# A hybrid attention and DeltaNet layer on one core: PSUM banks by turns, the solve in quarters, rotation tables in the keys, TensorE in source order in the heads

## Chip, core and metric

The kernel runs on one core of one Trainium2 chip. Times are device microseconds of that core. A core has five engines that run side by side and wait for each other by semaphores: TensorE (PE; its weight loads are shown as PEld), VectorE (DVE), ScalarE (ACT), GpSimd (POOL) and SyncE (SP), whose queue issues all DMAs here.

## What is computed

One decoder layer for 512 tokens of width 2048, all in float32:

```python
h = rms_norm(x, norm_w) * (1.0 + scale) + shift        # scale, shift, gate from silu(c) @ w_ada
aq, ak, av, ag, d_qkv, dz, db, da, mg_a, mg_b = split(h @ w_in)
# windowed attention: 32 query heads, 4 key heads of 64, rotation of the first 16 channels, sinks
y_a = (swa_attention(rope(norm(aq)), rope(norm(ak)), av, sinks) * silu(ag)) @ w_o_swa
# gated DeltaNet: 16 key heads, 32 value heads of 128, chunks of 64
dq, dk, dv = split(causal_conv_silu(d_qkv, conv_w))
t_inv = triangular_solve(eye + L, eye)                 # L = strict lower part of (beta k) k^T * decay
v_new = t_inv @ v_beta - (t_inv @ k_beta_decayed) @ S  # scan over chunks, state S
y_b = (rms_norm(o, dn_norm_w) * silu(dz)) @ w_o_dn
out = x + gate * ((sigmoid(mg_a) * y_a + sigmoid(mg_b) * y_b) @ w_out)
```

## The kernel before

It is written in a tile language: the program is a sequence of instructions in source order, and a planner puts each engine's instructions in an order of its own. It takes, of the instructions whose inputs it believes ready by its own estimate of times, the earliest in the source; it also picks the buffer of a pool that it believes free first. On the chip each engine then runs its list in that fixed order and waits where something is not ready. An explicit order between two instructions of one engine can be added (the method `behind` does that for single instructions).

Stages, in order, with their rough place in the profile: startup (norm and adaLN, first projections, to 130 us), **keys** (`delta_keys`: 12 more key tiles of the DeltaNet and 18 tiles of its output gate z, to about 535), **attention** (to about 1100), **heads** (`delta_heads`: 16 groups of one q tile, two v tiles and in seven of them a z tile, with the scans, to about 2000), and the **tail** (six 2048-wide products done by a seven-product scheme).

A *channel tile* (`channel_tile`) is 128 channels of `h @ w_in`: 16 steps of three matmuls of 512 columns (`mm3`, L276 to L278: high and low halves of the float32 operands) into one PSUM bank that `product_bank` gives. Weights come as 1 MB DMAs (`raw`), ACT rounds them (`whi`, L68) and DVE takes the rest (`wlo`, L69). Before, the pool `pmm` has two banks and the planner picks which one a tile gets; in the tail `pmm` and a second pool of two alternate.

All other work is in generators. `pump` is called after every second step of a channel tile, so eight times a tile. It advances them: a *live* generator yields the number of calls until its next step; a *paced* one gets a budget per call and yields what its next step costs. The names used later:

- `keys` (per key head): convolution by ACT (L650) and three DVE steps (L653, the last reader of the bank, `y`), transposes `ptk`, norm, transposes `ptkT`, ACT copy `kT` (L765), products `pkk` (L772), DVE mask times `E`. Key tiles and z tiles alternate from key 8 on.
- `z_gate`: ACT tanh into `zth` (L316), DVE product (L318, the last reader of the bank), store `z_d` (L320). `zth` has one buffer in the keys.
- `solve` (twice, for 16 heads each, paced 0.36): loads A, one DVE product over all of A (128x4096, L827), 124 DVE steps (L835, L843), eight ACT copies `atmp` with stores `ta_d`, one more product over A (L855), stores `ts_d`. At group 8 of the heads `drain_slow` runs what is left of it at once.
- `rope_tables`: sine and cosine tables by 20 DVE operations and two ACT `Sin`, run in one go at the start of attention, in whose key tiles (`key_pair`) ACT squares `ksq` for the product `kss`.
- `queries` (per group): convolution `yq`, loads of E and `kT`, transposes `ptq`, loads `qe`, `tt`, `ta`, `lab`, `ts1` (shown as `ts`), products `pqk` (L934), `py` (L942), ACT copy `Y`, products `pu`, then `scan`: per chunk `pp`, `pv`, `pod`, then transposes `pto`. `values` transposes v (`ptv`), which ACT copies to `vt`.
- `weight_sums`: sums of weight quarters for the tail on DVE (L1490), loads `q`, stores `s_d`.

Of the kernel before, what the change touches and what calls it, by code (L numbers as in the profile page):

```python
# [16 lines left out]
P = 128  # L17
# [35 lines left out]
class Layer:  # L53
# [218 lines left out]

    def mm3(self, ps, w, x, first, last):
        nc = self.nc
        (wh, wl), (xh, xl) = w, x
        nc.tensor.matmul(ps, lhsT=wh, rhs=xh, start=first, stop=False)  # L276
        nc.tensor.matmul(ps, lhsT=wh, rhs=xl, start=False, stop=False)  # L277
        self.last_mm = nc.tensor.matmul(ps, lhsT=wl, rhs=xh, start=False, stop=last)  # L278
# [43 lines left out]
    def transpose4(self, dst, src_cols):  # L322

        for c in range(4):
            self.nc.tensor.transpose(dst[:, c * P : (c + 1) * P], src_cols(c), self.ident)


    def build(self):
        tc, nc, a = self.tc, self.nc, self.a
        with ExitStack() as es:  # L330
            self.const = es.enter_context(tc.tile_pool(name="const", bufs=1))
            self.dram = es.enter_context(tc.tile_pool(name="scratch", bufs=1, space=DRAM))
            self.dnc_es = ExitStack()
            self.dnc = self.dnc_es.enter_context(tc.tile_pool(name="dnc", bufs=1, side="right"))
            self.v_d = self.dram.tile([2, P, T], F32, name="v_d")
            self.s_d = [self.dram.tile([2, 4, 2, P, 2048], F32, name=f"s_d{e}") for e in range(6)]
            self.gate_d = self.dram.tile([D], F32, name="gate_d")
# [22 lines left out]
            self.delta_keys()  # L360
            self.psc_es.close()
            self.attention()
            self.delta_heads()
            self.dnc_es.close()
# [30 lines left out]
    def startup(self, st):  # L395
# [54 lines left out]
        ada = self.pmm.tile([P, T], F32, tag="mm", name="ada")  # L450
# [94 lines left out]
        acc_ba = self.pmm.tile([P, T], F32, tag="mm", name="ba")  # L545
# [117 lines left out]
    def delta_keys(self):  # L663
# [9 lines left out]
        with ExitStack() as sa:  # L673
# [67 lines left out]
    def keys(self, wk, g, ps):  # L741
# [28 lines left out]
        for c in range(NTB):  # L770
            sl = slice(c * P, (c + 1) * P)
            nc.tensor.matmul(pk[:, c, :], lhsT=kT[:, sl], rhs=kT[:, sl], start=True, stop=True)  # L772
# [35 lines left out]
    def solve(self, wk, b, eng):  # L808
# [18 lines left out]
        self.behind(eng.tensor_tensor(out=A, in0=A, in1=nb.unsqueeze(1).to_broadcast([P, HD, HD]), op=ALU.mult))  # L827
# [27 lines left out]
        self.behind(eng.tensor_tensor(out=A, in0=A, in1=bet.unsqueeze(2).to_broadcast([P, HD, HD]), op=ALU.mult))  # L855
# [26 lines left out]
    def queries(self, wk, g, ps, st):  # L882
# [50 lines left out]
        for c in range(NTB):  # L933
            nc.tensor.matmul(pqk[:, c, :], lhsT=kT[:, sl(c)], rhs=q[:, sl(c)], start=True, stop=True)  # L934
# [5 lines left out]
        for c in range(NTB):  # L940
            for e in range(2):
                nc.tensor.matmul(py[own[1 - e], c, :], lhsT=lab[own[e], c, :], rhs=ta[own[e], c, :], start=True, stop=True)  # L942
# [4 lines left out]
        for c in range(NTB):  # L947
            nc.tensor.matmul(pu[0][0:HD, c, :], lhsT=Y[HD:P, c, :], rhs=TT[0][HD:P, c, HD:P], start=True, stop=True)
            nc.tensor.matmul(pu[1][0:HD, c, :], lhsT=Y[0:HD, c, :], rhs=ts1[0:HD, c, :], start=True, stop=True)
# [13 lines left out]
    def scan(self, wk, g, k, kT, TT, qd, M, epsq, st):  # L963
# [6 lines left out]
        for c in range(NTB):  # L970
            if c:
                pp = self.psc.tile([P, 4, P], F32, tag="sc", name="pp")[:, 0:2, :]
                nc.tensor.matmul(pp, lhsT=kT[:, sl(c)], rhs=S, start=True, stop=True)
# [8 lines left out]
            for e in range(2):  # L982
                nc.tensor.matmul(pv[:, e, :], lhsT=TT[e][:, c, :], rhs=r[:, e, :] if c else v[e][:, c, :], start=True, stop=True)  # L983
# [11 lines left out]
            if c < NTB - 1:  # L995
                nc.tensor.matmul(pd, lhsT=k[:, c, :], rhs=vs, start=True, stop=True)
            for e in range(2):
                if c:
                    nc.tensor.matmul(po[:, e, :], lhsT=qd[e][:, c, :], rhs=S[:, e, :], start=True, stop=False)
                nc.tensor.matmul(po[:, e, :], lhsT=M[e][:, c, :], rhs=vn[:, e, :], start=c == 0, stop=True)  # L1000
# [548 lines left out]
    def rope_tables(self, wk, keep):  # L1549
# [4 lines left out]
        nc.sync.dma_start(out=fr, in_=a["k_freq"])  # L1554
        ang = wk.tile([P, T], F32, tag="r1", name="ang", bufs=1)
        nc.vector.tensor_copy(out=ang, in_=posi)
        nc.vector.tensor_scalar(out=ang, in0=ang, scalar1=fr, scalar2=None, op0=ALU.mult)
        n = wk.tile([P, T], F32, tag="r2", name="turns", bufs=1)
        ni = wk.tile([P, T], I32, tag="r0", name="turni", bufs=1)
        nc.vector.tensor_scalar(out=n, in0=ang, scalar1=1.0 / (2 * math.pi), scalar2=None, op0=ALU.mult)  # L1560
        nc.vector.tensor_copy(out=ni, in_=n)
        nc.vector.tensor_copy(out=n, in_=ni)
        for part in (TWO_PI_HI, TWO_PI_MID, TWO_PI_LO):
            nc.vector.scalar_tensor_tensor(out=ang, in0=n, scalar=-part, in1=ang, op0=ALU.mult, op1=ALU.add)

        def wrap(t):
            for lim, cmp, by in ((math.pi, ALU.is_gt, -2 * math.pi), (-math.pi, ALU.is_lt, 2 * math.pi)):
                nc.vector.tensor_scalar(out=n, in0=t, scalar1=lim, scalar2=by, op0=cmp, op1=ALU.mult)
                nc.vector.tensor_tensor(out=t, in0=t, in1=n, op=ALU.add)
            nc.vector.tensor_scalar(out=t, in0=t, scalar1=3.1415925, scalar2=-3.1415925, op0=ALU.min, op1=ALU.max)  # L1570

        wrap(ang)
        self.sin = keep.tile([P, T], F32, name="sin")
        self.cos = keep.tile([P, T], F32, name="cos")
        nc.scalar.activation(self.sin, ang, AF.Sin)
        sg = keep.tile([P, 1], F32, name="sgn")
        nc.sync.dma_start(out=sg, in_=a["k_sgn"])
        nc.vector.tensor_scalar(out=self.sin, in0=self.sin, scalar1=sg, scalar2=None, op0=ALU.mult)
        nc.vector.tensor_scalar(out=ang, in0=ang, scalar1=math.pi / 2, scalar2=None, op0=ALU.add)
        wrap(ang)  # L1580
        nc.scalar.activation(self.cos, ang, AF.Sin)
# [14 lines left out]
    def attention(self):  # L1596
        tc, nc, a = self.tc, self.nc, self.a
        with ExitStack() as es:
# [47 lines left out]
    def value_tokens(self, t, i):  # L1646
        pt = self.ptp.tile([P, NTB, P], F32, tag="tp", name="ptva")
        for c in range(NTB):
            self.nc.tensor.transpose(pt[:, c, :], t[:, c * P : (c + 1) * P], self.ident)
# [5 lines left out]
    def key_pair(self, rwk, t, ps, blk, kw, kd):  # L1655
# [8 lines left out]
        nc.tensor.matmul(pss, lhsT=blk, rhs=sq, start=True, stop=True)  # L1664
# [41 lines left out]
    def scales(self, wk, sqs, blk, rs):  # L1706
# [3 lines left out]
        for c in range(NTB):  # L1710
            sl = slice(c * P, (c + 1) * P)
            for p in range(4):
                nc.tensor.matmul(pt[32 * p : 32 * p + 32, sl], lhsT=blk[:, 48:80], rhs=sqs[p][:, sl], start=True, stop=True)
# [4 lines left out]
        for c in range(NTB):  # L1718
            nc.tensor.transpose(pt[:, c, :], sb[:, c * P : (c + 1) * P], self.ident)
# [7 lines left out]
    def attend(self, wk, kd, n, mask, sink, qs, rs, sg, done):  # L1727
        nc = self.nc
        for i in range(NTB):
# [5 lines left out]
            for pp in range(2):  # L1735
# [5 lines left out]
                for j in range(2):  # L1741
                    for e, (ps, t) in enumerate(tl):
# [3 lines left out]
                        if i == 0:  # L1746
                            nc.tensor.matmul(ps[:, j, P:], lhsT=q[b, isl], rhs=kd[b, 0:P], start=True, stop=True)
                            continue
                        for u in range(2):
                            rr = slice(u * HD, (u + 1) * HD)  # L1750
                            o = u * HD
                            nc.tensor.matmul(
                                ps[rr, j, HD - o : 256 - o], lhsT=q[b, i * P + o : i * P + o + HD],
                                rhs=kd[b, (i - 1) * P + o : (i - 1) * P + o + 192], start=True, stop=True,
                            )
# [70 lines left out]
    def gate(self, wk):  # L1826
# [17 lines left out]
        for c in range(4):  # L1844
            sl = slice(c * T, (c + 1) * T)
            ps = self.ptp.tile([P, T], F32, tag="tp", name="pgate")
            nc.tensor.matmul(ps, lhsT=self.ones, rhs=acc[:, sl], start=True, stop=True)
# [88 lines left out]
```

## Time and profile before

| | |
|---|---|
| Median of 3 runs | 2913.75 us (2908.66 to 2920.05) |
| The profiled execution | 2917.7 us |
| Its span, first to last instruction | 2915.9 us |
| TensorE busy | 2797.7 us (96%) |
| DVE, ACT, POOL busy | 2218.9, 1318.3, 147.3 us |
| DMA | 776 MB, mean 266 GB/s |

Times in the profile count from the first instruction. A row of a timeline gives start, duration, engine, source line, operation, output<-inputs, shape, count and, in brackets, the idle time of the engine before it with what ended it. Matmuls are pipelined and their ends are modelled, so a busy TensorE can still be slow: the granted clock says how slow.

### The profile page before, as it was taken

Reading aid. Unit: us, or ns where it says so; the run is one execution under the profiler, and the core shown is the slowest. Engines: PE = TensorE matmul, PEld = TensorE weight load, DVE = VectorE, ACT = ScalarE, POOL = GpSimd, SP = SyncE. Lnnn points to the kernel's source line nnn. Section 1 sums busy time; section 2 is a strip of 40 time slices with the busy share of each in tenths; the row PEclk is TensorE's granted clock in tenths of the full one; section 3 lists DMA queues with packets and bytes.
Section 4 is the critical chain, followed back from the end, with each engine's and each line's share of the span. In section 5 each row is a group of like instructions: output and inputs, shape, how many; then the busy total and the mean of one; then the engine's idle time right before and its main releaser. Section 6 shows DMA issues by size and latency. Waiting matters only on the chain.

```text
span 2915.9 us, 39613 instructions
## 1 busy us (share of the span) xinstructions
PE 2797.7 (96%) x13864; PEld 2246.0 (77%) x13864; DVE 2218.9 (76%) x3582; ACT 1318.3 (45%) x2647; POOL 147.3 (5%) x124
## 2 busy tenths in 40 slices
PE   8999898899999999999998999989999999999999
PEld 6788676777777778888886777867878878788887
DVE  7877787787786778889876776768766868887876
ACT  5565342234454444444453434435544645454543
POOL 0000000010000001101100100110000000000000
PEclk9999999999999999999999999999999999999999
DMA  9889788454456558999979998876789989998865
GB/s 402 336 275 292 264 270 300 142 177 155 157 172 185 175 164 287 290 306 300 294 236 289 314 302 274 293 228 230 247 292 326 318 323 329 350 346 276 297 242 195
DMA packets 332651, 776.38 MB, mean 266 GB/s; under 512 B 88066, under 2 KB 112258, under 8 KB 287394
## 3 DMA queue, kind: packets, MB, share of 16 engines
q1 hardware_dynamic: 332452, 773.86, 79.0%
q8 instruction: 109, 1.79, 0.2%
q14 instruction: 90, 0.74, 0.1%
HBM read 588.84 MB, written 182.66 MB: 265 GB/s over the span
## 4 chain that ended last, share of the span: by engine, by line
PE 71%; DMA 11%; DVE 10%; ACT 3%; issue 3%; SPq 1%; POOL 0%; DVEq 0%; ACTq 0%; POOLq 0%
PE mm L276 12%; PE mm L278 11%; PE mm L277 11%; PE m L277 9%; PE m L278 9%; PE m L276 8%; DMA s_d<-q 2%; DVE wlo L69 2%; DMA q<-in_w_q 2%; DMA raw<-in_w_ch 1%; DMA b_d<-o 1%; DVE q L1490 1%; PE O L1815 1%; PE pv L983 1%; PE pod L1000 1%
## 5 line engine op out<-in xcount | busy, mean ns | idle before, releaser
L69 DVE TENSOR_TENSOR wlo<-raw,whi 128x1024 fp32r<-128x1024 f32 x588 | 721.4, 1231 | 336.1 <-ACT whi L68 325.5
L68 ACT CAST whi<-raw 128x1024 fp32r<-128x1024 f32 x588 | 614.9, 1051 | 722.7 <-PE m L278 346.9
L276 PE MATMUL mm<-hh,whi 128*128 128x512 f32 x2016 | 823.4, 408 | 27.3 <-DVE zth L318 8.8
L278 PE MATMUL mm<-hh,wlo 128*128 128x512 f32 x2016 | 804.7, 399 | 6.5 <-DVE wlo L69 6.5
L277 PE MATMUL mm<-hl,whi 128*128 128x512 f32 x2016 | 803.0, 398 | 0.0
L276 PEld LDWEIGHTS mm<-hh,whi 128*128 128x128 f32 x2016 | 384.9, 191 | 120.0 <-issue 22.8
L278 PEld LDWEIGHTS mm<-hh,wlo 128*128 128x128 f32 x2016 | 384.0, 190 | 92.5 <-DVE wlo L69 10.3
L277 PEld LDWEIGHTS mm<-hl,whi 128*128 128x128 f32 x2016 | 385.5, 191 | 74.6 <-issue 1.6
L1490 DVE TENSOR_TENSOR q<-q,q 128x512 f32<-128x512 f32 x384 | 277.9, 724 | 15.9 <-DMA q<-in_w_q 14.5
L800 POOL TENSOR_SCALAR_AFFINE_SELECT E<-E 128x512 f32<-128x512 f32 x64 | 56.6, 893 | 1073.8 <-DMA E<-g_rows 962.2
L843 DVE TENSOR_TENSOR A<-A,atmp 128x62 f32<-128x62 f32 (+30 forms) x124 | 108.9, 878 | 0.6
L835 DVE TENSOR_TENSOR atmp<-A 128x62 f32<-128x62 f32 (+30 forms) x124 | 107.5, 867 | 0.5
L806 ACT ACTIVATE E<-E,neg_g 128x128 f32<-128x128 f32 x256 | 80.1, 394 | 28.2 <-POOL E L800 28.2
L653 DVE SCALAR_TENSOR_TENSOR yv<-mm,convh,yv 128x511 f32<-128x511 f32 (+2 forms) x96 | 71.5, 744 | 24.6 <-ACT yv L650 23.6
L277 PE MATMUL m<-wlo,hh 128*128 128x512 f32 x192 | 77.0, 401 | 5.2 <-DVE wlo L69 5.2
L276 PE MATMUL m<-whi,hh 128*128 128x512 f32 x192 | 76.7, 401 | 2.7 <-ACT whi L68 2.7
L278 PE MATMUL m<-whi,hl 128*128 128x512 f32 x192 | 76.1, 396 | 0.0
L988 ACT ACTIVATE vs<-pv,kd 128x128 f32<-128x128 f32 x96 | 30.1, 365 | 90.5 <-PE pv L983 90.3
L277 PE MATMUL m<-wlo,f2h 128*128 128x512 f32 x160 | 62.6, 391 | 1.2 <-DVE wlo L69 1.2
L276 PE MATMUL m<-whi,f1h 128*128 128x512 f32 x160 | 62.7, 392 | 0.0
L278 PE MATMUL m<-whi,f0l 128*128 128x512 f32 x160 | 62.5, 390 | 0.0
L278 PE MATMUL m<-whi,f2l 128*128 128x512 f32 x160 | 62.4, 390 | 0.0
(431 smaller groups left out, 4774.5 us busy)
## 6 DMA issues: line engine op xcount, KB each, us to landing
raw<-in_w_ch SPq DMA_DIRECT2D x126, 1024.0 KB
q<-in_w_q SPq DMA_DIRECT2D x384, 256.0 KB
s_d<-q SPq DMA_DIRECT2D x384, 256.0 KB
raw<-s_d SPq DMA_DIRECT2D x96, 1024.0 KB
raw<-in_w_q SPq DMA_DIRECT2D x72, 1024.0 KB
wa<-in_w_ada_ss SPq DMA_DIRECT2D x32, 1024.0 KB
gw<-in_w_ada_gate SPq DMA_DIRECT2D x16, 1024.0 KB
E<-g_rows SPq DMA_DIRECT2D x64, 256.0 KB
```

The source lines that it names most:

```text
L68: h = self.nc.scalar.copy(out=hi, in_=src)
L69: l = self.nc.vector.tensor_tensor(out=lo, in0=src, in1=hi.bitcast(F32), op=ALU.subtract)
L276: nc.tensor.matmul(ps, lhsT=wh, rhs=xh, start=first, stop=False)
L277: nc.tensor.matmul(ps, lhsT=wh, rhs=xl, start=False, stop=False)
L278: self.last_mm = nc.tensor.matmul(ps, lhsT=wl, rhs=xh, start=False, stop=last)
L653: nc.vector.scalar_tensor_tensor(out=y[:, s:], in0=ps[:, : T - s], scalar=w[:, j : j + 1], in1=y[:, s:], op0=ALU.mult, op1=ALU.add)
L800: self.last_mask = self.nc.gpsimd.affine_select(out=E, in_=E, pattern=[[0, NTB], [1, P]], compare_op=ALU.is_ge, fill=NEG, base=0, channel_ ...
L806: self.nc.scalar.activation(E[:, c, :], E[:, c, :], AF.Exp, bias=self.neg_g[:, c, h : h + 1])
L835: eng.tensor_tensor(out=t, in0=A[:, m : m + 1, m + 1 :].to_broadcast([P, m, n]), in1=A[:, :m, m : m + 1].to_broadcast([P, m, n]), op=ALU.mult,
L843: self.behind(eng.tensor_tensor(out=A[:, :m, m + 1 :], in0=A[:, :m, m + 1 :], in1=t, op=ALU.add))
L988: nc.scalar.activation(vs[:, e, :], pv[:, e, :], AF.Copy, scale=self.kd[:, c, 2 * g + e : 2 * g + e + 1])
L1490: self.behind(self.nc.vector.tensor_tensor(out=q[f], in0=q[x], in1=q[y], op=ALU.add))
```

## The change

Four edits. **Banks:** the two-bank pool becomes pools of one bank that products take strictly by turns; in the tail four of them.

```diff
-            self.pmm = pm_es.enter_context(tc.tile_pool(name="pmm", bufs=2, space=PSUM, reuse_waits="tile"))
-            self.banks, self.bank_i = [self.pmm], 0
+            bank = lambda n: pm_es.enter_context(tc.tile_pool(name=f"pm{n}", bufs=1, space=PSUM, reuse_waits="tile"))
+            self.banks, self.bank_i = [bank(0), bank(1)], 0
...
-            self.banks.append(self.pmb)
+            self.banks += [bank(2), bank(3)]
```

**Solve:** the two products over A are made in four parts, each followed by a yield of 1.2 (the second alike), and the pace is 0.41.

```diff
-            self.solves = self.paced(self.solve_all(), 0.36)
+            self.solves = self.paced(self.solve_all(), 0.41)
...
-        self.behind(eng.tensor_tensor(out=A, in0=A, in1=nb.unsqueeze(1).to_broadcast([P, HD, HD]), op=ALU.mult))
+        for j in range(0, HD, 16):
+            s = slice(j, j + 16)
+            self.behind(eng.tensor_tensor(out=A[:, s], in0=A[:, s], in1=nb.unsqueeze(1).to_broadcast([P, 16, HD]), op=ALU.mult))
+            yield 1.2
```

**Rotation tables:** `sin` and `cos` get a pool of their own around keys and attention; the tables are made by a live generator in the keys that begins after 40 calls of the pump. Its steps are one or two DVE operations with yields of 2 between them; the last steps are the two ACT `Sin` and the sign.

```diff
+            rwk = sa.enter_context(tc.tile_pool(name="rwk", bufs=1, reuse_waits="tile"))
+            self.go(self.rope_tables(rwk, rwk), 40)
...
-            with ExitStack() as er:
-                rwk = er.enter_context(tc.tile_pool(name="rwk", bufs=1, reuse_waits="tile"))
-                self.rope_tables(rwk, keep)
```

**Source order:** every matmul and transpose goes through `pe`, which in the heads, and there alone, adds an order behind the instruction before it in the source on TensorE.

```diff
+    def pe(self, ins):
+        return self.tc.keep_in_program_order(ins) if self.in_order else ins
...
-        nc.tensor.matmul(ps, lhsT=wh, rhs=xh, start=first, stop=False)
+        self.pe(nc.tensor.matmul(ps, lhsT=wh, rhs=xh, start=first, stop=False))
...
+            self.in_order = True
             self.delta_heads()
+            self.in_order = False
```

More of the change, by code (lines that the diff above doesn't have):

```diff
@@ L275, in mm3 @@
         (wh, wl), (xh, xl) = w, x
-        nc.tensor.matmul(ps, lhsT=wh, rhs=xh, start=first, stop=False)
-        nc.tensor.matmul(ps, lhsT=wh, rhs=xl, start=False, stop=False)
-        self.last_mm = nc.tensor.matmul(ps, lhsT=wl, rhs=xh, start=False, stop=last)
+        self.pe(nc.tensor.matmul(ps, lhsT=wh, rhs=xh, start=first, stop=False))
+        self.pe(nc.tensor.matmul(ps, lhsT=wh, rhs=xl, start=False, stop=False))
+        self.last_mm = self.pe(nc.tensor.matmul(ps, lhsT=wl, rhs=xh, start=False, stop=last))
     def behind(self, ins, other=None):
@@ L324, in transpose4 @@
         for c in range(4):
-            self.nc.tensor.transpose(dst[:, c * P : (c + 1) * P], src_cols(c), self.ident)
+            self.pe(self.nc.tensor.transpose(dst[:, c * P : (c + 1) * P], src_cols(c), self.ident))
     def build(self):
@@ L359, in build @@
             self.sol = self.dnc_es.enter_context(tc.tile_pool(name="sol", bufs=1, side="right", reuse_waits="tile"))
-            self.delta_keys()
-            self.psc_es.close()
-            self.attention()
+            with tc.tile_pool(name="rope", bufs=1) as rope:
+                self.sin, self.cos = (rope.tile([P, T], F32, name=n) for n in ("sin", "cos"))
+                self.delta_keys()
+                self.psc_es.close()
+                self.attention()
+            self.in_order = True
             self.delta_heads()
+            self.in_order = False
             self.dnc_es.close()
@@ L449, in startup @@
         ssq = sp.tile([P, NTB], F32, name="xssq")
-        ada = self.pmm.tile([P, T], F32, tag="mm", name="ada")
+        ada = self.product_bank("ada")
         by_pe = lambda kt: int(kt % 2 == 0 or kt == KT - 1)
@@ L544, in startup @@
         acc_v = [pa.tile([P, T], F32, tag=f"x{i}", name=f"v{i}") for i in range(2)]
-        acc_ba = self.pmm.tile([P, T], F32, tag="mm", name="ba")
+        acc_ba = self.product_bank("ba")
         self.acc_k = [self.psc.tile([P, T], F32, tag="sc", name=f"k{n}") for n in range(NST)]
@@ L771, in keys @@
             sl = slice(c * P, (c + 1) * P)
-            nc.tensor.matmul(pk[:, c, :], lhsT=kT[:, sl], rhs=kT[:, sl], start=True, stop=True)
+            self.pe(nc.tensor.matmul(pk[:, c, :], lhsT=kT[:, sl], rhs=kT[:, sl], start=True, stop=True))
         nc.sync.dma_start(out=self.kT_d[g], in_=kT)
@@ L854, in solve @@
         yield 4.5
-        self.behind(eng.tensor_tensor(out=A, in0=A, in1=bet.unsqueeze(2).to_broadcast([P, HD, HD]), op=ALU.mult))
+        for j in range(0, HD, 16):
+            s = slice(j, j + 16)
+            self.behind(
+                eng.tensor_tensor(
+                    out=A[:, s], in0=A[:, s], in1=bet[:, s].unsqueeze(2).to_broadcast([P, 16, HD]), op=ALU.mult
+                )
+            )
+            yield 1.2
         for k2 in range(2):
@@ L933, in queries @@
         for c in range(NTB):
-            nc.tensor.matmul(pqk[:, c, :], lhsT=kT[:, sl(c)], rhs=q[:, sl(c)], start=True, stop=True)
+            self.pe(nc.tensor.matmul(pqk[:, c, :], lhsT=kT[:, sl(c)], rhs=q[:, sl(c)], start=True, stop=True))
         for e in range(2):
@@ L941, in queries @@
             for e in range(2):
-                nc.tensor.matmul(py[own[1 - e], c, :], lhsT=lab[own[e], c, :], rhs=ta[own[e], c, :], start=True, stop=True)
+                self.pe(nc.tensor.matmul(py[own[1 - e], c, :], lhsT=lab[own[e], c, :], rhs=ta[own[e], c, :], start=True, stop=True))
         Y = wk.tile([P, NTB, HD], F32, tag="Y", name="Y", bufs=1)
@@ L947, in queries @@
         for c in range(NTB):
-            nc.tensor.matmul(pu[0][0:HD, c, :], lhsT=Y[HD:P, c, :], rhs=TT[0][HD:P, c, HD:P], start=True, stop=True)
-            nc.tensor.matmul(pu[1][0:HD, c, :], lhsT=Y[0:HD, c, :], rhs=ts1[0:HD, c, :], start=True, stop=True)
+            self.pe(nc.tensor.matmul(pu[0][0:HD, c, :], lhsT=Y[HD:P, c, :], rhs=TT[0][HD:P, c, HD:P], start=True, stop=True))
+            self.pe(nc.tensor.matmul(pu[1][0:HD, c, :], lhsT=Y[0:HD, c, :], rhs=ts1[0:HD, c, :], start=True, stop=True))
         for e in range(2):
@@ L972, in scan @@
                 pp = self.psc.tile([P, 4, P], F32, tag="sc", name="pp")[:, 0:2, :]
-                nc.tensor.matmul(pp, lhsT=kT[:, sl(c)], rhs=S, start=True, stop=True)
+                self.pe(nc.tensor.matmul(pp, lhsT=kT[:, sl(c)], rhs=S, start=True, stop=True))
                 r = wk.tile([P, 2, P], F32, tag="r", name="r", bufs=1)
@@ L982, in scan @@
             for e in range(2):
-                nc.tensor.matmul(pv[:, e, :], lhsT=TT[e][:, c, :], rhs=r[:, e, :] if c else v[e][:, c, :], start=True, stop=True)
+                self.pe(nc.tensor.matmul(pv[:, e, :], lhsT=TT[e][:, c, :], rhs=r[:, e, :] if c else v[e][:, c, :], start=True, stop=True))
             vn = wk.tile([P, 2, P], F32, tag="vn", name="vn", bufs=2)
@@ L995, in scan @@
             if c < NTB - 1:
[L996 removed]
+                self.pe(nc.tensor.matmul(pd, lhsT=k[:, c, :], rhs=vs, start=True, stop=True))
             for e in range(2):
                 if c:
[L999 to L1000 removed]
+                    self.pe(nc.tensor.matmul(po[:, e, :], lhsT=qd[e][:, c, :], rhs=S[:, e, :], start=True, stop=False))
+                self.pe(nc.tensor.matmul(po[:, e, :], lhsT=M[e][:, c, :], rhs=vn[:, e, :], start=c == 0, stop=True))
             nc.scalar.copy(out=osb[:, :, c, :], in_=po)
@@ L1554, in rope_tables @@
         nc.sync.dma_start(out=fr, in_=a["k_freq"])
+        sg = keep.tile([P, 1], F32, name="sgn")
+        nc.sync.dma_start(out=sg, in_=a["k_sgn"])
+        yield 4
         ang = wk.tile([P, T], F32, tag="r1", name="ang", bufs=1)
@@ L1561, in rope_tables @@
         nc.vector.tensor_copy(out=ni, in_=n)
+        yield 2
         nc.vector.tensor_copy(out=n, in_=ni)
@@ L1569, in wrap @@
                 nc.vector.tensor_tensor(out=t, in0=t, in1=n, op=ALU.add)
+                yield 2
             nc.vector.tensor_scalar(out=t, in0=t, scalar1=3.1415925, scalar2=-3.1415925, op0=ALU.min, op1=ALU.max)
-        wrap(ang)
-        self.sin = keep.tile([P, T], F32, name="sin")
-        self.cos = keep.tile([P, T], F32, name="cos")
+            yield 2
+        yield from wrap(ang)
+        nc.vector.tensor_scalar(out=self.cos, in0=ang, scalar1=math.pi / 2, scalar2=None, op0=ALU.add)
+        yield from wrap(self.cos)
+        yield 3
         nc.scalar.activation(self.sin, ang, AF.Sin)
-        sg = keep.tile([P, 1], F32, name="sgn")
-        nc.sync.dma_start(out=sg, in_=a["k_sgn"])
+        nc.scalar.activation(self.cos, self.cos, AF.Sin)
+        yield 2
         nc.vector.tensor_scalar(out=self.sin, in0=self.sin, scalar1=sg, scalar2=None, op0=ALU.mult)
-        nc.vector.tensor_scalar(out=ang, in0=ang, scalar1=math.pi / 2, scalar2=None, op0=ALU.add)
-        wrap(ang)
-        nc.scalar.activation(self.cos, ang, AF.Sin)
     def rope(self, x, i):
@@ L1648, in value_tokens @@
         for c in range(NTB):
-            self.nc.tensor.transpose(pt[:, c, :], t[:, c * P : (c + 1) * P], self.ident)
+            self.pe(self.nc.tensor.transpose(pt[:, c, :], t[:, c * P : (c + 1) * P], self.ident))
         vt = self.vtok_a[:, :, i * P : (i + 1) * P]
@@ L1663, in key_pair @@
         pss = self.ptp.tile([P, T], F32, tag="tp", name="kss")
-        nc.tensor.matmul(pss, lhsT=blk, rhs=sq, start=True, stop=True)
+        self.pe(nc.tensor.matmul(pss, lhsT=blk, rhs=sq, start=True, stop=True))
         ms = rwk.tile([P, T], F32, tag="pT", name="kms", bufs=4)
@@ L1712, in scales @@
             for p in range(4):
-                nc.tensor.matmul(pt[32 * p : 32 * p + 32, sl], lhsT=blk[:, 48:80], rhs=sqs[p][:, sl], start=True, stop=True)
+                self.pe(nc.tensor.matmul(pt[32 * p : 32 * p + 32, sl], lhsT=blk[:, 48:80], rhs=sqs[p][:, sl], start=True, stop=True))
         sb = wk.tile([P, T], F32, tag="th", name="ssb", bufs=1)
@@ L1718, in scales @@
         for c in range(NTB):
-            nc.tensor.transpose(pt[:, c, :], sb[:, c * P : (c + 1) * P], self.ident)
+            self.pe(nc.tensor.transpose(pt[:, c, :], sb[:, c * P : (c + 1) * P], self.ident))
         ss = wk.tile([P, NTB, 8], F32, tag="ss", name="ss", bufs=1)
@@ L1746, in attend @@
                         if i == 0:
-                            nc.tensor.matmul(ps[:, j, P:], lhsT=q[b, isl], rhs=kd[b, 0:P], start=True, stop=True)
+                            self.pe(nc.tensor.matmul(ps[:, j, P:], lhsT=q[b, isl], rhs=kd[b, 0:P], start=True, stop=True))
                             continue
@@ L1846, in gate @@
             ps = self.ptp.tile([P, T], F32, tag="tp", name="pgate")
-            nc.tensor.matmul(ps, lhsT=self.ones, rhs=acc[:, sl], start=True, stop=True)
+            self.pe(nc.tensor.matmul(ps, lhsT=self.ones, rhs=acc[:, sl], start=True, stop=True))
             nc.vector.tensor_tensor(out=acc[:, sl], in0=ps, in1=b[:, sl], op=ALU.add)
```

10 lines of the change are left out of this document (6 added, 4 removed).

## The prediction

> **What bounds the kernel now.** I read the summary of busy time first, then the busy time by stretches, then what TensorE waited for, then the timelines at the places that these name.
>
> ```profile
> span 2915.9 us, 39613 instructions
> PE 2797.7 (96%) x13864; PEld 2246.0 (77%) x13864; DVE 2218.9 (76%) x3582; ACT 1318.3 (45%) x2647; POOL 147.3 (5%) x124
> ```
>
> TensorE is the bound, so only what keeps it idle or slow can be won. The table by stretches has, after the stretch: its length, busy time of PE, PEld, DVE, ACT, POOL with instruction counts, the granted TensorE clock, the DMA share and GB/s.
>
> ```profile
> 130.00:300.00 170.00, 169.22 (x832) 139.94 (x831) 124.04 (x244) 94.17 (x266) 11.45 (x18) 1.00 0.90 282
> 300.00:520.00 220.00, 191.84 (x807) 151.99 (x806) 165.48 (x246) 75.19 (x176) 14.29 (x16) 0.93 0.82 275
> 520.00:600.00 80.00, 72.31 (x310) 58.28 (x309) 62.85 (x85) 20.43 (x25) 8.30 (x3) 0.96 0.40 127
> 600.00:1200.00 600.00, 587.47 (x3111) 449.26 (x3110) 469.32 (x918) 256.13 (x596) 39.08 (x27) 1.00 0.60 191
> 1200.00:1550.00 350.00, 346.33 (x1882) 284.19 (x1880) 297.36 (x511) 161.48 (x428) 34.36 (x24) 1.00 0.88 285
> 1550.00:1600.00 50.00, 41.50 (x204) 32.86 (x203) 26.55 (x43) 16.73 (x43) 3.85 (x4) 0.86 0.91 294
> 1600.00:2000.00 400.00, 371.93 (x1986) 300.17 (x1985) 276.29 (x498) 163.50 (x449) 35.77 (x28) 0.97 0.85 275
> ```
>
> I count a stretch's loss as its idle time plus (1 - clock) times its length. Keys, 300 to 520: 28.2 + 15.4 = 43.6 us. Start of attention, 520 to 600: 7.7 + 3.2 = 10.9. First part of the heads, 1200 to 1550: 3.7, or 1% of its length. Then 1550 to 1600: 8.5 + 7.0 = 15.5, and 1600 to 2000: 28.1 + 12.0 = 40.1. Together 114 us; what the change can win is in them.
>
> **Banks by turns (keys).** What TensorE waited for (us in total, times, longest):
>
> ```profile
> PE mm L276 <- DVE zth L318: 8.8, 3, 5.8
> PE mm L276 <- DVE y L653: 6.0, 5, 3.1
> PE pkk L772 <- ACT kT L765: 4.6, 6, 0.8
> ```
>
> The timeline of TensorE at one of the five waits for y, and the busy time of a stretch just behind it:
>
> ```profile
> 376.56 0.60 PE L325 MATMUL ptkT<-ident,k 128*128 128x128 f32 x4
> 377.98 1.16 PE L772 MATMUL pkk<-kT 128*128 128x128 f32 x8 [0.82 <-ACT kT L765]
> 379.86 0.50 PE L276 MATMUL mm<-hh,whi 128*128 128x512 f32 x1 [0.72 <-DVE y L653]
> 380.89 0.63 PE L276 MATMUL mm<-hh,whi 128*128 128x512 f32 x1
> 380.50:383.50 3.00, 3.00 (x9) 2.32 (x8) 2.40 (x4) 3.00 (x11) 0.00 (x0) 0.50 0.76 317
> ```
>
> A z tile starts as soon as the convolution has read the last bank (y), though two banks exist: it was put into the bank that the key tile had just filled. So the next product cannot start, the order brings ptkT and pkk back to back with nothing between, and TensorE idles 0.82 + 0.72 us; then nine matmuls run at a granted clock of 0.50, which costs another 1.5 us of 3.0. That is 3.0 us a time. The five waits total 6.0 with one of 3.1, so four are of this kind: 12 us, and the fifth gives 3.1.
>
> [...]
>
> Against this stands why the banks repeat:
>
> ```profile
> 309.83 0.69 ACT L650 ACTIVATE y<-mm,convh 128x512 f32<-128x512 f32 x1 [10.70 <-PE mm L278]
> 332.99 0.59 ACT L316 ACTIVATE zth<-mm 128x512 f32<-128x512 f32 x1
> 312.00 4.42 DVE L827 TENSOR_TENSOR A<-A,nbet 128x4096 f32<-128x4096 f32 x1
> ```
>
> The z tile computed before this key tile is read 23 us after it: its copy has one buffer (zth), which waits for a store in SP's queue. Strict turns make the next z tile wait for that late reader. So waits for zth can replace those for y. Reading z takes ACT only 0.59 us, and with TensorE held, ACT and DVE are free to do it; I put the new waits at half of today's 8.8, or 4.4. Net: 12 + 3.1 - 4.4 = 10.7 us. Bounds: -14 (each of five z tiles waits 5.8 as in the longest row, 29 us, against the 15.1 won) to +24 (all 8.8 of z waits go as well). In the tail two pools of two banks become four banks in the same rotation: nothing, within 2 us either way.
>
> **Solve in quarters at 0.41.** The 4.42 us multiplication at 312 held the convolution behind it on DVE; quarters of 1.1 us let others in between. It is the cause of the 3.1 us counted above, so it gets nothing more. The pace matters at the end. From the yields one solve needs 131 units, or 364 calls of the pump at 0.36; with eight more yields of 1.2 it needs 141, or 343 at 0.41. Counted out, the second solve ends at call 782 before and 741 after; the heads force the rest out at group 8, call 752. Before, 30 calls' worth is thrown out at once:
>
> ```profile
> 1526.84 2.09 ACT L849 COPY atmp<-A 64x512 f32<-64x512 f32 x2
> 1528.97 4.42 DVE L855 TENSOR_TENSOR A<-A,bet 128x4096 f32<-128x4096 f32 x1 [2.57 <-ACT atmp L849]
> 1537.03 9.13 SPq L1495 DMA_DIRECT2D s_d<-q  x4
> 1560.37 1.16 PE L934 MATMUL pqk<-yq,kT 128*128 128x128 f32 x8 [2.51 <-DMA kT<-kT_d]
> ```
>
> The stores of T and the 4.42 us op fall together, SP's queue stalls 9 us on four stores, and TensorE waits for kT. Afterwards it ends 11 calls early, so the burst goes. Of 15.5 us, 0.5 is normal; the DMA share there is 0.91, so I take two thirds: 10 us (0 to 15). The faster pace puts 14% more of the solve's DVE work beside keys and attention, where TensorE idles 12.5 us of 600 with DVE at 78%: -3 (-8 to 0).
>
> **Rotation tables in the keys.** At the start of attention:
>
> ```profile
> 546.83 0.48 DVE L1557 TENSOR_SCALAR ang<-ang,freq 128x512 f32<-128x512 f32 x1
> 562.05 0.43 DVE L1570 TENSOR_SCALAR ang<-ang 128x512 f32<-128x512 f32 x1
> 556.86 1.28 ACT L1575 ACT_TABLE_LOAD   x1
> 562.51 0.63 ACT L1581 ACTIVATE cos<-ang 128x512 f32<-128x512 f32 x1 [3.73 <-DVE ang L1570]
> 563.04 0.58 ACT L1659 ACTIVATE ksq<-mm 128x512 f32<-128x512 f32 x1
> 563.67 2.08 PE L1664 MATMUL kss<-ksq,blk 128*128 128x512 f32 x2 [7.69 <-ACT ksq L1659]
> ```
>
> ACT sits in cos, which waits for the chain on DVE, and ksq, the reader of the first attention key tile, is queued behind it: TensorE waits 7.69 us, and the clock loses 3.2. With the tables done, ksq comes right behind its tile: +10.9. In the keys the same 20 DVE operations (the first and last are shown; at 0.5 us each about 10 us), two table loads of 1.28 us on ACT and three DMAs on SP come into 130 to 300, where TensorE idles 0.8 us of 170 and DVE is 73% busy. They come in steps of two, about 1 us. What is queued behind the first (ang, which waits for the positions to land) is DVE's wlo; SP may be late there. I take -2 (-8 to 0). Net 9.
>
> **TensorE in source order in the heads.** Rows in order of time (the last is from the table of waits) show the way from the reading of a q tile to the load of kT, and to py, in an early group and a late one:
>
> ```profile
> 1204.66 0.68 ACT L650 ACTIVATE yq<-mm,convh 128x512 f32<-128x512 f32 x1
> 1217.64 0.42 SPq L890 DMA_DIRECT2D kT<-kT_d  x1
> 1234.08 0.60 SPq L920 DMA_DIRECT2D ts<-ts_d  x1
> 1237.57 0.33 PE L942 MATMUL py<-ta,lab 64*64 64x64 f32 x2
> 1679.24 0.69 ACT L650 ACTIVATE yq<-mm,convh 128x512 f32<-128x512 f32 x1 [3.69 <-PE mm L278]
> 1717.47 0.47 SPq L890 DMA_DIRECT2D kT<-kT_d  x1
> 1747.54 0.33 PE L942 MATMUL py<-ta,lab 64*64 64x64 f32 x2
> 1732.63 0.59 ACT L879 COPY vt<-ptv 128x512 f32<-128x512 f32 x1 [5.78 <-PE ptv L325]
> 1739.39 0.77 PE L276 MATMUL mm<-hh,whi 128*128 128x512 f32 x1 [3.12 <-DVE yq L653]
> ACT Y L944 <- PE py L942: 65.0, 15, 11.8
> ```
>
> 13 and 33 us early, 38 and 68 us late: the big products have run ahead of the small steps. ACT waited 65.0 us in all for py alone. In the late group it stands 5.78 us at a copy whose transposes come late in TensorE's order, what is behind it (the convolution, the splits) is late, and TensorE pays 3.12 us at a bank. Source order forbids running ahead, so this kind goes; the tail's products are not held, so they can still fill the end of the last scan. If 1600 to 2000 came to the 1% of the first part, it would win 40.1 - 4 = 36. The price is that TensorE now stands at each small step that is not ready. Nearest row: in the early group py starts 3.5 us after the issue of the last load, so it is about as early as loads allow, and the code puts it seven calls (some 13 us) behind the step that issues nine loads of 0.6 us. I take 1.5 us a group, 16 groups: -24. Bounds: 0, and 5 us plus 1.7 of clock a group, -107. Net 12 (-71 to +36).
>
> **The sum.** 10.7 + 10 - 3 + 9 + 12 = 39 us off the profiled execution's 2917.7 is 2879; that execution lies 4 us above the median of the runs, 2913.75, so I forecast 2875.
>
> **The rivals.** (1) Slower: TensorE in order stands at py, pu and the scan for SP's loads in every group. Without any such wait the change would win 63 us; 63 / 16 = 3.9 us a group eats it, above 4.9 it is slower by over 0.5%. At 6.7 a group it is 107 - 63 = 44 us slower: 2958. For: DMA share 0.88 and kT 13 us behind its q tile even early. Against: 3.7 us of idle in 350 near source order. Chance 0.12. (2) The heads are bound by DMA and SP: the order only moves the waits, and the burst's transfers remain. The terms 10 and 12 fall away: 17 us, 2897. Chance 0.17. (3) Strict turns turn y waits into z waits, so the keys win nothing: 28 us, 2886; with (2) together 6 us, 2908. Chance 0.11 alone, 0.13 together. (4) Everything comes: 24 + 15 + 11 + 36, less the 5 of pace and tables, is 81: 2833. Chance 0.10. My forecast keeps 0.37, within 2855 to 2893.
>
> 0.5% of 2914, or 15 us, is about what a measurement of this kernel tells from no change. Faster by that (below 2899): 0.37 + 0.10 + 0.11 and, as 2897 is so near the line, 0.13 of case 2: 0.71. Same: 0.04 + 0.13 = 0.17. Slower: 0.12. The range is 2840 to 2915: it leaves out the slower case and half of case 4.
>
> **What would show it.** Right: no TensorE wait for y L653 in the keys and no waits for zth beyond 4 us; kss without a wait; no copies of atmp bunched in the heads and kT of group 8 some 15 us behind its q tile; ACT's waits for py (65.0 us now) and ptv mostly gone, and short new waits of TensorE at py and pu; clock 0.97 or better in every stretch after 300. Wrong: TensorE waits for DMA ta, tt or kT in most groups, or for zth at each z tile, with the clock at 0.5 behind them.

## The result and the profile after

The changed kernel took 2880.12 us (median of 4 runs) against 2911.2 before: ratio 0.9885, 95% interval [0.9868, 0.9901]. In a second comparison, on another occasion, it took 2872.49 against 2911.99: 0.9857 [0.9842, 0.9872]. So it gained 31 and 39.5 us. The forecast was 2875 and a sum of 39 us. The profiled execution of the changed kernel took 2872.4 us, the shortest of its first four, and that of before, 2917.7, is near the top of its own: the two traces differ by 45 us, which is 14 and 6 us more than the medians of the two comparisons.

The table by stretches of the changed kernel, with the columns of the one before:

```profile
130.00:300.00 170.00, 168.02 (x826) 138.62 (x826) 131.03 (x261) 100.01 (x270) 14.49 (x18) 1.00 0.88 280
300.00:520.00 220.00, 190.97 (x831) 153.76 (x830) 172.82 (x258) 77.04 (x182) 14.54 (x16) 0.94 0.84 284
520.00:600.00 80.00, 80.00 (x375) 64.93 (x377) 67.01 (x77) 21.66 (x27) 9.19 (x5) 1.00 0.54 170
1200.00:1550.00 350.00, 337.17 (x1860) 277.80 (x1859) 282.23 (x502) 158.12 (x418) 33.29 (x28) 0.99 0.94 306
1550.00:1600.00 50.00, 49.81 (x282) 41.37 (x280) 37.03 (x68) 20.69 (x58) 3.85 (x4) 1.00 0.90 290
1600.00:2000.00 400.00, 381.20 (x2020) 314.85 (x2018) 282.00 (x519) 181.98 (x465) 27.15 (x24) 0.97 0.82 267
```

Read as before (idle time plus the clock's share): the keys lose 42.2 us, as good as the 43.6 before; the start of attention loses nothing (10.9 before); 1200 to 1550 loses 16.3 (3.7 before), 1550 to 1600 0.2 (15.5) and 1600 to 2000 30.8 (40.1). The work in a stretch has moved a little, since the kernel is shorter, but the pattern is plain: won at attention's start, around 1575 and, less, behind 1600; lost in the first half of the heads; nothing won in the keys.

What TensorE waited for, changed kernel:

```profile
PE mm L280 <- DVE zth L322: 12.9, 4, 5.8
PE pp L994 <- DVE S L1029: 11.1, 10, 2.7
PE ptk L329 <- DVE E L786: 8.7, 1, 8.7
PE py L963 <- DMA lab<-lab_d: 5.1, 2, 3.3
PE pkk L783 <- ACT kT L776: 4.7, 5, 1.7
```

The waits for y (6.0 us) have gone. In their place stand 4.1 us more of zth (8.8 before; the longest, 5.8, stood there before too) and a wait of 8.7 us for an E product (1.1 before): the keys have traded.

### The profile page after: what moved, and what is told of

Its sections match the earlier page's. It is cut to its first block, busy times and chain, and to the rows that moved or that the text cites. A ratio compares the mean times of both kernels' runs of the same rounds, so it can differ in the third digit from the quotient of the medians.

```text
span 2870.7 us, 39644 instructions
## 1 busy us (share of the span) xinstructions
PE 2769.7 (96%) x13864; PEld 2237.7 (78%) x13864; DVE 2212.2 (77%) x3594; ACT 1318.3 (46%) x2649; POOL 139.6 (5%) x124
## 4 chain that ended last, share of the span: by engine, by line
PE 44%; DMA 7%; DVE 3%; issue 1%; SPq 1%; ACT 1%; POOL 0%; DVEq 0%; POOLq 0%; ACTq 0%
PE m L281 9%; PE m L282 9%; PE m L280 9%; PE mm L280 4%; PE mm L282 4%; PE mm L281 4%; DMA s_d<-q 3%; DMA q<-in_w_q 1%; DVE wlo L69 1%; PE pv L1004 1%; PE pp L994 1%; PE pod L1021 1%; DMA b_d<-o 0%; PE pod L1017 0%; PE pod L1020 0%
## 5 line engine op out<-in xcount | busy, mean ns | idle before, releaser
L280 PE MATMUL mm<-hh,whi 128*128 128x512 f32 x2016 | 832.0, 413 | 12.9 <-DVE zth L322 12.9
L282 PE MATMUL mm<-hh,wlo 128*128 128x512 f32 x2016 | 795.1, 394 | 0.0
L281 PE MATMUL mm<-hl,whi 128*128 128x512 f32 x2016 | 792.9, 393 | 0.0
L1511 DVE TENSOR_TENSOR q<-q,q 128x512 f32<-128x512 f32 x384 | 270.5, 704 | 48.0 <-DMA q<-in_w_q 34.5
L817 ACT ACTIVATE E<-E,neg_g 128x128 f32<-128x128 f32 x256 | 82.2, 400 | 16.3 <-POOL E L811 13.2
L1022 ACT COPY osb<-pod 128x256 f32<-128x256 f32 x64 | 23.7, 371 | 117.2 <-PE pod L1021 93.1
L1807 ACT ACTIVATE sm<-sm,mx,rs 128x128 f32<-128x128 f32 x128 | 61.5, 482 | 2.9 <-DVE mx L1802 2.4
```

Of the source, the lines that this page charges most:

```text
L280: self.pe(nc.tensor.matmul(ps, lhsT=wh, rhs=xh, start=first, stop=False))
L281: self.pe(nc.tensor.matmul(ps, lhsT=wh, rhs=xl, start=False, stop=False))
L282: self.last_mm = self.pe(nc.tensor.matmul(ps, lhsT=wl, rhs=xh, start=False, stop=last))
L817: self.nc.scalar.activation(E[:, c, :], E[:, c, :], AF.Exp, bias=self.neg_g[:, c, h : h + 1])
L1511: self.behind(self.nc.vector.tensor_tensor(out=q[f], in0=q[x], in1=q[y], op=ALU.add))
L1807: nc.scalar.activation(t, t, AF.Exp, scale=r[:, h : h + 1], bias=mx[:, h : h + 1], accum_out=den[:, h : h + 1])
```

## The experiments

All times of the experiments are medians; the kernel before took 2912 in the first two sets and 2915.7 in the third. To say where time went I mark in each trace the first matmul of attention's first tile, of the heads' first q tile, of group 8's, and of the tail. The keys are counted from 122.5 us on, where their first product starts in most traces (up to 1.9 us later in the others). Groups 0 to 7 have 27 channel tiles, groups 8 to 15 have 28. The rows from a_banks to a_order are the four edits alone, the others are described under the headings below. The lengths (us):

| kernel | keys | attention | groups 0-7 | groups 8-15 | tail | median | ratio to before |
|---|---|---|---|---|---|---|---|
| before | 410.6 | 562.1 | 389.1 | 461.7 | 970.0 | 2912 | 1 |
| changed, first trace | 406.5 | 543.8 | 397.9 | 438.2 | 961.8 | 2880.1 | 0.9885 |
| again | 407.0 | 543.2 | 395.9 | 434.1 | 970.5 | 2872.5 | 0.9857 [0.9842, 0.9872] |
| a_banks | 411.9 | 559.2 | 389.8 | 460.9 | 975.3 | 2922.0 | 1.0034 [1.0022, 1.0046] |
| a_solve | 407.3 | 556.8 | 388.1 | 450.3 | 976.9 | 2903.7 | 0.9965 [0.9953, 0.9978] |
| a_rope | 407.3 | 547.9 | 388.5 | 455.8 | 976.7 | 2900.4 | 0.9951 [0.9937, 0.9966] |
| a_order | 410.1 | 563.1 | 396.7 | 447.1 | 963.2 | 2896.9 | 0.9943 [0.9925, 0.9961] |
| no_turns | 406.7 | 544.4 | 393.7 | 435.8 | 964.1 | 2872.2 | 0.9860 [0.9846, 0.9873] |
| order_from_8 | 408.2 | 545.9 | 401.6 | 449.5 | 965.0 | 2894.5 | 0.9938 [0.9925, 0.9950] |
| order_to_8 | 407.0 | 545.3 | 394.1 | 427.2 | 977.9 | 2876.9 | 0.9875 [0.9858, 0.9892] |
| turns_zth2 | 407.6 | 564.1 | 390.4 | 462.4 | 976.5 | 2925.3 | 1.0045 [1.0032, 1.0058] |
| keys_turns | 415.4 | 564.4 | 387.7 | 456.8 | 973.6 | 2917.0 | 1.0009 [0.9997, 1.0021] |
| pace_only | 409.3 | 556.3 | 397.0 | 460.3 | 972.3 | 2917.2 | 1.0004 [0.9993, 1.0014] |
| gw_pool | 423.5 | 543.3 | 397.6 | 438.1 | 971.6 | 2894.1 | 0.9928 [0.9912, 0.9944] |

Rows two and three are the same program: its tail differs by 8.7 us between two executions, its groups 8 to 15 by 4, groups 0 to 7 by 2, its keys and attention by less than 1. Stage lengths behind 1500 us are good to some 9 us, no better; the verdicts rest on the medians.

### Each edit alone, on the kernel before

**Banks by turns** (`banks = [bank(0), bank(1)]`, four in the tail).

> The kernel before with the banks by turns alone. By the prediction's term: 10.7 us faster (2900 against 2911), no wait of TensorE for y of a key tile left, waits for zth about 4 us. Rival, from the two traces (the keys as a whole ended only 4 us earlier in the changed kernel, with 12.9 us of waits for zth): the turns trade one wait for the other, 0 to 4 us faster (2907 to 2911). A third: the tail is 8 us shorter in the changed trace; if four banks in one turn are the cause, up to 8 us of the gain lies behind 1950 us.

Measured: 10.0 us slower; neither theory. The keys, 411.9 us, are as long as before, so the turns traded waits there, as the rival had it. The largest, with TensorE first, then ACT and DVE:

```profile
330.69 0.69 PE L329 MATMUL ptk<-ident,y 128*128 128x128 f32 x2 [14.58 <-DVE E L782]
321.14 0.58 ACT L320 ACTIVATE zth<-mm 128x512 f32<-128x512 f32 x1
327.08 2.35 DVE L1846 SCALAR_TENSOR_TENSOR gate_bc<-gw,silu_c,gate_bc 128x2048 f32<-128x2048 f32 x1
329.35 1.28 DVE L782 TENSOR_TENSOR E<-pkk,E 128x512 f32<-128x512 f32 x2
330.55 0.68 DVE L322 SCALAR_TENSOR_TENSOR zth<-zth,mm 128x512 f32<-128x512 f32 x1
```

The z tile that follows must take the other bank, and the last reader of that bank (zth, L322) is on DVE, in DVE's own order behind gate_bc and the E products: ACT has read z by 321.7, DVE, busy without a gap from 311.7 on, gets to it at 330.6. Before, this z tile took the bank just read and started at 317; now it starts at 331. The 10 us themselves are not in the keys: at the tail's first product this trace is 1.6 us ahead of the one before, and its tail is 5.3 longer, within the tail's scatter. The two profiled executions differ by 3.7 us only, so most of the 10 us does not show in them.

**Solve in quarters at 0.41** (`0.36 -> 0.41`, both products in four).

> The kernel before with the solve in quarters at 0.41 alone. By the prediction: the burst at 1530 to 1600 us goes (10 us), the faster pace costs 3: 7 us faster (2904). Rival, from the traces: between 1550 and 1600 us the changed kernel wins 17 us on the one before, and if all of that is the burst, 14 us faster (2897). Second rival: the end of the solve only moves its stores to 1450 us, beside other groups, and nothing is won (2911).

Measured: 8.3 us faster, nearer the prediction's term than either rival. Between 1450 and 1600 us TensorE idles 4.3 us, where it idled 10.0 before, and no wait for kT is left.

**Rotation tables in the keys** (`self.go(self.rope_tables(rwk, rwk), 40)`).

> The kernel before with the rotation tables made in the keys alone. By the prediction: the wait for ksq of 7.7 us and its slow clock go (10.9 us), the keys lose 2: 9 us faster (2902), no loss between 540 and 580 us. Rival, from the traces: attention's start is 16 us shorter in the changed kernel, with 6 us of it behind the first key tiles: 14 to 16 us faster (2896). Second rival: the steps in the keys delay SP and DVE there by 2 to 8 us and eat half: 2906.

Measured: 11.6 us faster, between the forecast and the first rival. Attention is 14 us shorter, the keys are no longer than before. ksq and kss in the changed kernel:

```profile
541.26 0.60 ACT L1683 ACTIVATE ksq<-mm 128x512 f32<-128x512 f32 x1
543.53 1.02 PE L1688 MATMUL kss<-ksq,blk 128*128 128x512 f32 x2
553.52 0.59 ACT L1683 ACTIVATE ksq<-mm 128x512 f32<-128x512 f32 x1
```

ksq comes behind its tile; kss carries no bracket, so TensorE did not wait.

**Source order in the heads** (`self.in_order = True` around `delta_heads`).

> The kernel before with TensorE in source order in the heads alone. By the prediction: 12 us faster (2899), the work behind a q tile comes early and the groups wait for no bunched copies. Rival, from the traces: the first half of the heads (1140 to 1530 us) is 20 us longer in the changed kernel, from more waits in a fixed order, and the second half wins about 10 beside the burst: 5 to 10 us slower (2916 to 2921). Second rival: the two halves cancel, within 5 us of 2911.

Measured: 15.1 us faster. The rival had the sign of the first half right (7.6 us lost in groups 0 to 7, not 20) and drew the wrong sum: 14.6 come back in groups 8 to 15, and the tail is shorter by 6.8 (more on the tail under "Source order in groups 0 to 7 alone"). The new waits of a fixed order are there:

```profile
PE pto L329 <- DVE osb L1039: 17.4, 6, 4.1
PE pp L980 <- DVE S L1015: 12.6, 10, 4.2
PE py L949 <- DMA lab<-lab_d: 8.2, 3, 6.1
```

The four alone sum to -25.0 us; the three without the banks to -35.0.

### The changed kernel with one thing altered

> The changed kernel itself, once more, as the mark for the three others of this call: 2880 us by its first four runs.

Measured: 2872.5.

**The pool of two put back** (`self.banks = [self.pmm]`, the rest kept).

> The changed kernel with the pool of two banks put back, the other three edits kept. The banks by turns alone cost 10 us. If edits add up: 10 us faster than the changed kernel, 2870. Rival, the prediction's term of 10.7 us holds beside the other three edits, which take the long wait of 14.6 us at 331 us away (8.7 in the changed kernel): 2885 to 2891. Second rival: the 10 us of the single edit lie in the tail's four banks, then the tail behind 1950 us is the part that gets shorter.

Measured: 2872.2, the same as the changed kernel in the same set. None of the three: as far as these runs can tell (to some 4 us) the turns give nothing and cost nothing here. The three other edits make the whole gain, 39.8 us.

**Source order from group 8 on.**

```diff
-            self.in_order = True
             self.delta_heads()
...
             for g in range(KH):
+                self.in_order = g >= 8
```

> The changed kernel with TensorE in source order only from group 8 of the heads on, the planner's order in groups 0 to 7. With the edit alone the tiles of the first groups come 7 us later, and those up to the end of the solve 10 more, and all of its gain lies behind 1580 us. If the halves are independent: 8 to 18 us faster than the changed kernel, 2862 to 2872. Rival: the lag that the planner's order builds up in the first groups must first be there to be won back, so what is won early is lost at the switch: 2880. Second rival: slower, because the solve's end and the late stores collide in groups 6 to 8 without the early reads: 2885 to 2890.

Measured: 2894.5, 22 us slower than the changed kernel, worse than any theory. TensorE at the switch:

```profile
1475.64 2.07 PE L955 MATMUL pqk<-yq,kT 128*128 128x128 f32 x8 [4.69 <-DMA kT<-kT_d]
1495.08 0.44 PE L963 MATMUL py<-ta,lab 64*64 64x64 f32 x2 [11.71 <-DMA lab<-lab_d]
1497.01 1.09 PE L963 MATMUL py<-ta,lab 64*64 64x64 f32 x14 [1.49 <-DMA lab<-lab_d]
```

In group 7 the load of kT is issued 34 us behind the reading of its q tile (7.8 us in the changed kernel). Source order makes TensorE stand until SP has caught up. This is the mechanism of the prediction's first rival, an in-order TensorE that waits for SP's loads; in these runs it shows only where a lag was already there.

**Source order in groups 0 to 7 alone** (`g < 8`).

> The changed kernel with TensorE in source order only in groups 0 to 7 of the heads, the planner's order from group 8 on. If the gain of source order lies in the second half (32 us behind 1580 us in the trace of the single edit): the loss of the first half stays and the gain goes, 2887 to 2900. If the 23 us that source order from group 8 on lost at the switch mean that the gain is made by keeping step early: 2870 to 2877.

Measured: 2876.9, within the uncertainty of the changed kernel. Without any source order it would take some 2892 (an estimate: 2912 less the 8.3 and 11.6 us that the solve and the tables win alone), so nearly the whole gain of source order is made without it in the second half. From group 8 on the lag builds up again; group 11:

```profile
1643.95 0.69 ACT L658 ACTIVATE yq<-mm,convh 128x512 f32<-128x512 f32 x1 [5.08 <-PE mm L282]
1677.07 0.42 SPq L911 DMA_DIRECT2D kT<-kT_d  x1
```

33 us, nearly as large as before (38). Yet groups 8 to 15 take only 427.2 us. So a lag is not itself the loss.

One reading would be that time is borrowed: big products run ahead, and the small steps are left for later. A count of the heads' small matmuls (all but the channel tiles', 1856 in every trace) bears this out in part:

- When group 8 begins, the kernel before has done 784 of them and the changed kernel 796. The 12 are some 2 us of TensorE's time (an estimate, by the 1.16 us that eight of them, pqk, take at 1560 us in the trace before), so most of the 7.6 us that source order alone costs in the first half is no loan; it is in waits: TensorE idles 11.4 us there instead of 3.7.
- When the tail begins, 108 are left in every trace with the planner's order from group 8 on, this one too, and 72 in every trace with source order there. The tail then takes 970.0 to 977.9 us in the eight traces of the first kind and 961.8 to 971.6 in the six of the second. So part of what looks like scatter of the tail goes with this, and groups 8 to 15 with the tail come to 1405.1 us here, against 1404.6 in the row "again".

In groups 8 to 15 TensorE idles 8.7 us here, and its granted clock is 1.00 from 1550 to 1600 us and 0.98 from 1600 to 2000, the last 104 us of which are the tail's; the kernel before idles 27.7 us there and loses 13.7 to the clock. Why they run so well, with the lag growing again, is not shown.

### Inside the edits

**Two buffers for zth beside the turns** (`"zth", 1 -> 2`, on a_banks).

> The kernel before with banks by turns, and two buffers instead of one for the copy zth in the keys. If z tiles are read late because the copy's one buffer waits for its store: the waits for zth of the single edit (12.9 us, and the 14.6 us at 331 us) go, 15 to 25 us faster than the single edit's 2922, 2897 to 2907. Rival: the reader is late because DVE has E products, weight sums and gate_bc ahead of its step in its own order: the same waits, 2918 to 2922.

Measured: 2925.3. At the long wait the mechanism of the first theory held: with a second buffer z is read in time. Its time did not come:

```profile
330.50 0.66 PE L329 MATMUL ptk<-ident,y 128*128 128x128 f32 x4 [1.29 <-DVE E L782]
334.09 0.50 PE L280 MATMUL mm<-hh,whi 128*128 128x512 f32 x1 [2.93 <-ACT whi L68]
336.51 0.79 PE L282 MATMUL mm<-hh,wlo 128*128 128x512 f32 x1 [1.55 <-DVE wlo L69]
```

The 14.6 us fell to 1.3, but weights are late next, the waits for zth fell only from 12.9 to 7.3, and the wait at attention's start grew:

```profile
PE mm L280 <- DVE zth L322: 7.3, 2, 6.9
PE kss L1671 <- ACT ksq L1666: 11.1, 1, 11.1
```

The keys end 4.3 us sooner than with turns alone, and attention is 4.9 longer: ksq, queued behind the rotation tables, starts at 564.6 us here and at 564.8 with turns alone, so TensorE waits there for what the keys had won. Two buffers in the changed kernel, whose tables are made earlier, were not tried.

**Turns in startup and keys alone**: after the keys the two pools are closed and a pool of two is opened.

> The kernel before with the banks by turns in the startup and the keys alone; from attention on the pool of two, in the tail two pools of two as before. If the 10 us of the single edit lie in the keys: 2920 to 2922. If the keys only shift their waits and the cost lies in the heads or in the tail's four banks: 2912, as before.

Measured: ratio 1.0009 [0.9997, 1.0021], no clear change. So at most a part of the 10 us of a_banks comes from the keys; where the rest comes from, attention, heads or tail, is open: the late stages scatter by as much.

**The pace alone**, products whole.

> The kernel before with the solve's pace at 0.41 and its two products over A whole. By the prediction all of the solve's gain is the burst that the pace takes away, less 3 us for the pace: the same as with the quarters, 2902 to 2905. Rival: the quarters bring some 3 us of their own (the convolution behind the 4.42 us product at 312 us): 2907. Second rival: without the quarters the pace alone costs, 2912 or more.

Measured: ratio 1.0004; the second rival comes nearest. The solve now ends at 1398 us instead of 1534, the burst at 1560 to 1590 is smaller, and the loss lies earlier, in two new waits for yq at 1466 (5.5 us) and 1519 (3.3); the other two stand much as before:

```profile
PE mm L280 <- DVE yq L660: 14.4, 4, 5.5
```

Groups 0 to 7 take 397.0 us instead of 389.1. Between 1450 and 1600 us TensorE idles 11.8 us, as much as before (10.0). So the pace alone does not make the gain; with the quarters (a_solve) groups 0 to 7 take 388.1. The quarters also bring yields of their own, so that at the same pace the solve's last stores come at 1481 us instead of 1398: whether the smaller operations or the later end make the gain is not separated. Quarters without the pace were not tried.

**gw loaded by POOL's queue** (`nc.sync -> nc.gpsimd`, on the changed kernel).

> The changed kernel with the 1 MB loads of the output gate's weights (gw) issued by POOL's queue instead of SP's. In the keys SP stands 22 to 30 us in waits for gate_bc on these loads, up to 13 us at once, with the weight loads raw behind them. If SP's queue, and not TensorE's banks, sets the pace of the keys: the waits for raw and the late stores z_d shrink, 8 to 20 us faster than the changed kernel (2852 to 2864). Rival: the waits for zth stay, since DVE's order sets them, and the keys end where they did: 2870 to 2875. Second rival: POOL's own work (the masks of E) is held by the loads: 2880 or more.

Measured: 2894.1, the time of the second rival. POOL stands in the waits that SP had, and its masks of E behind them:

```profile
POOL gw L1856 <- DVE gate_bc L1863: 76.5, 8, 12.5
130.00:300.00 170.00, 149.37 (x704) 122.01 (x702) 127.34 (x236) 87.88 (x236) 21.53 (x33) 0.94 0.88 290
```

TensorE idles 20.6 us between 130 and 300, where the changed kernel idles 2.0. The masks are not the only way there: DVE stands 38.6 us (11 times) for the loads of gw between 125 and 320, with the steps that TensorE needs behind it; in the changed kernel's keys it waits for one 0.6 us once. The two are not separated. Half of the 35 us lost by 310 comes back by 475, but the others could catch up in the stalls, so whether SP's queue alone sets the pace of the keys stays open.

## Why the prediction was right, and where it was not

**The sum** (39 us) was met in the second comparison (39.5; 31 in the first), and it was met by errors that cancel, which is luck: the banks gave nothing instead of 10.7, and the other three together 39.8 (no_turns) instead of the 28 that the forecast has for them.

**Banks, +10.7 forecast, -10 alone and 0 in the whole.** The small waits came as forecast: those for y went, and those for zth grew from 8.8 to 12.9 us, by 4.1 where the forecast has 4.4. The step that failed is "reading z takes ACT only 0.59 us, and with TensorE held, ACT and DVE are free to do it". At 331 us DVE was not free: z's last reader stood in DVE's own order behind steps that have nothing to do with it, and TensorE waited 14.6 us (8.7 in the whole, 1.1 before), a wait for which the sum has no term. The one buffer of zth is the other half of it: with two, 1.3 us are left of this wait. The clock's share of the term failed as well: the clock in 300 to 520 us is 0.93 before and 0.94 in the changed kernel, since it falls at the new waits instead (0.53 from 323 to 329 us, around the end of the wait of 8.7 us; 0.57 from 376 to 384, at one of 2.8 us for zth). The third rival (the keys win nothing) is what happened there; its time, 2886, did not come, because the other three gave more than it counted with. What a_banks lost outside the keys is not explained, and that the tail's four banks change nothing is neither shown nor refuted.

**Solve, +7 forecast, 8.3 measured.** The size was right and one step was not: "the burst goes" because of the pace, while the quarters get nothing. The pace alone gives nothing; it moves the solve's end to 1398 us, and between 1450 and 1600 us TensorE idles as much as it did with the burst.

**Rotation tables, +9 forecast, 11.6 measured.** The wait for ksq went as counted. The -2 for the keys was too much: they are no longer than before.

**Source order, +12 forecast, 15.1 measured.** The parts of the sum (36 won in the second half, 24 lost to waits) have the right signs and are both too large; the traces show 14.6 won in groups 8 to 15, 7.6 lost in groups 0 to 7, and the rest in the tail, for which fewer of the heads' matmuls are left. The mechanism came: in the changed kernel kT of group 8 follows its q tile at 10.0 us (52 before, 23.6 with source order alone, 38.0 with the solve alone), and ACT's wait for py fell from 65.0 us to:

```profile
ACT Y L965 <- PE py L963: 23.5, 8, 5.8
```

The waits for SP's loads at py stayed short (3.3 at most), so the first rival did not come. Nor did the 1.7 us of clock a group that it and the lower bound count with. One place in the trace before lost that much (a clock of 0.57 over the 4 us from 380 on), but no run shows it in every group: the heads of the changed kernel ran at a clock of 0.99 over their 836 us, a loss of under 1 us a group. What the forecast did not see is where the order has to stand: it reckoned the gain in the second half, but with the order in the first half alone the kernel is nearly as fast, and with the order from group 8 on alone it is 22 us slower.

**Marks set in advance.** No wait for y in the keys, kss without a wait, kT about 15 us behind (10.0), short new waits at py: right. ACT's waits for py "mostly gone": in part, a third is left. No wait for zth over 4 us and a clock of at least 0.97 in every stretch: wrong, with 5.8 us and 0.94 in the keys.

**A version that beats both** was not found: the changed kernel with its pool of two is as fast and simpler.

## What to carry to other kernels

Taking away an engine's longest wait wins its length only if nothing behind it comes late for another reason: the 14.6 us wait went, and the kernel was no faster, because it then waited for weights and for the rotation tables instead. Before costing strict turns of buffers, look up the reader that frees each buffer in its own engine's order, not only how long it takes. In this kernel program order on the bound engine cost little where the queue that feeds it kept step (7.6 us in 389), and a great deal when it was switched on after the queue had fallen behind (waits of 4.7 and 11.7 us at once).

## What the runs showed of the hardware

The forecast took 1.54 us of idle time as enough to halve TensorE's clock. In these traces the length alone does not decide. Of the four such places that it counted in the keys, each with 0.82 us of idle time and then 0.71 or 0.72, the clock fell behind three (0.57 from 380 to 384 us, 0.61 from 408 to 412, 0.57 from 435 to 439), and not behind the one at 354 (1.00 from 354 to 362). Two places of the changed kernel, each with the matmul that ended the idle time and the stretch around or behind it:

```profile
916.73 0.72 PE L329 MATMUL pP<-ident,sm 128*128 128x128 f32 x3 [2.10 <-DVE sm L1815]
916.00:920.00 4.00, 3.27 (x17) 2.62 (x18) 3.90 (x13) 2.98 (x5) 0.00 (x0) 1.00 0.29 79
1133.45 0.70 PE L994 MATMUL pp<-S,kT 128*128 128x256 f32 x2 [1.88 <-DVE S L1029]
1133.50:1137.00 3.50, 3.50 (x12) 2.92 (x13) 2.97 (x6) 1.47 (x8) 0.00 (x0) 0.60 0.64 143
```

2.10 us of idle left the clock at 1.00, 1.88 us took it to 0.60 over the next 3.5 us. What decided between them is not shown.

Also unexpected: two executions of one program agree within 1 us over their first 1100 us, then part by 6 us up to the tail, and by 8.7 the other way in it. Both leave 72 matmuls for the tail, so this part of the scatter has another cause, which is not known.
